# Mean squares of the first residual stream: squares on ScalarE alone, the sums inside TensorE's mean matmuls

## The chip, the cores and the metric

The kernel runs on one core of a Trainium2 chip. The metric is the device time of one execution, in microseconds, as a median over runs. Engines go by the profile's names: PE is TensorE (PEld its weight loads), DVE VectorE, ACT ScalarE, POOL GpSimd, and SP the engine whose queue issues most DMAs.

## The reference

Two decoder layers over 1024 tokens of width 1024, all in f32: the first mixes by differential attention, the second by causal pooling; both also attend to 256 memory tokens. What bears on the change is the normalisation ahead of the first layer.

```python
def rms_norm(x, g):
    xf = x.astype(jnp.float32)
    y = xf * lax.rsqrt(jnp.mean(xf * xf, axis=-1, keepdims=True) + EPS)
    return (y * g.astype(jnp.float32)).astype(x.dtype)
...
    h = x
    mem_n = rms_norm(mem, mem_norm_g)
    for i in range(DEPTH):
        hn = rms_norm(h, ln_g[i])
        ...
            proj = jnp.einsum('bsd,de->bse', hn, attn_w_in[j])
            ...
            y = diff_attention(u, positions, attn_lambda[j], attn_subln_g[j], lambda_init_fn(i))
        ...
        z = jnp.concatenate([y, m], axis=-1) * jax.nn.silu(gate)
        h = h + jnp.einsum('bse,ed->bsd', z, w_out[i])
    return rms_norm(h, final_g)
```

## The kernel before

Activations lie transposed: the model width is on the 128 partitions, in 8 tiles (`d` = 0 to 7), and the tokens are on the free axis in two halves of 512. Half 1 is worked first. Every f32 operand of a projection is split into a high part (`hh`, `wh_...`, made by ScalarE) and a low part (`hl`, `wl_...`, made by VectorE, or by GpSimd and VectorE for weights), and `mm3` issues three matmuls per 128 x 128 x 512 block: L126, L127, L128. A projection of one half is 24 such matmuls.

The row scale of the normalisation, 1/sqrt(mean square), is applied after the projections. So the prologue (`prologue`) does several things at once. It loads x into tiles `xf`, makes `hh` and `hl` of each (`new_hidden`, L498 and L499), and projects q and k of the first head in both halves, in the order k of half 1, q of half 1, k of half 0, q of half 0. It also squares each tile of x and sums the squares over `d` (`accumulate_square`), takes the means by matmuls against a column of 1/1024 (`mean_square`, L251: for each of four groups of 128 tokens one matmul per tile in its list, with one column of output), and forms the inverse root by three Newton steps of small VectorE operations (L225 to L242). The scale is spread over the partitions by matmuls (`row_spread`, L528), copied to `rsb` by ScalarE (L536), and multiplied into the cosine and sine tables (`spread`, L370 and L371). Then the held rotations of q and k run: L761 to L766, then the splits of `kb` (L800, L801) and of `qa` and `qlo` (L781 to L783).

The tables themselves are made in `rope_tables`: angles on VectorE, one sine pass on ScalarE (L560), a DMA to DRAM (L561) and eight DMAs back (L564). ScalarE needs a table load when it goes from sines to exponentials. `lambda_full` (L578 to L584) makes a coefficient for the attention with one exponential (L581).

In `accumulate_square` before, ScalarE squares a tile (L512) or an engine named by `by` does (L510), and the square is added to the first one of its half (L516) by GpSimd, or by VectorE for `d` above 3. In half 1 the last square stays apart (`alone`), so half 1 has a list of two tiles and half 0 a list of one.

The order on TensorE is written by hand (`manual_schedule`): the program order of matmuls is the order of execution. On the other engines and on the DMA queues a scheduler orders the instructions by simulated times, with `high_priority` for the Newton steps, and it orders the whole program anew when a part is changed. After the prologue, score blocks (L849), softmax, transposes and applied weights of twelve heads run interleaved with the projections of the next head, then the memory attention, the output projection, and the second layer.

Of the kernel before, what the change touches and what calls it, by code (L numbers as in the profile page):

```python
# [10 lines left out]
F32 = mybir.dt.float32  # L11
# [3 lines left out]
AF = mybir.ActivationFunctionType  # L15
# [5 lines left out]
P = 128  # L21
# [3 lines left out]
HALF = 512  # L25
# [23 lines left out]
class Trunk:  # L49
# [285 lines left out]
    def prologue(self, pool):  # L335

        nc, a = self.nc, self.a
        xs = {}
        raw = []
        sums = [[], []]  # L340
        w = {}
        held = []

        def load_x(half, c):
            x = pool.tile([P, 2, HALF], F32, tag="eb", bufs=5, name=f"xf{half}{c}")
            nc.sync.dma_start(x, a["x"][half, :, 2 * c : 2 * c + 2, :])
            xs[half, 2 * c], xs[half, 2 * c + 1] = x[:, 0, :], x[:, 1, :]

        def hidden(half, ks):
            for d in ks:  # L350
                self.new_hidden(half, d, xs[half, d], self.ln_g[0])
                self.accumulate_square(
                    pool, xs[half, d], sums[half], d, f"x{half}{d}",
                    (("sq", 2), ("og", 3), ("es", 4)), alone=half == 1, by=None if half else (None, nc.vector)[d % 2],
                    add=nc.vector if d > 3 else None,
                )

        def project(which, half, bank):
            def evac(half, out):
                fn = (self.query_evac, self.key_evac)[which]  # L360
                held.append((half, lambda: fn(0, self.qkv[0][which])(half, out)))

            for _ in self.project(w[which], half, f"{'qk'[which]}0", evac, bank):
                pass

        def spread(half):
            self.keep_spread(half)
            cols = slice(half * HALF, (half + 1) * HALF)
            c, s, r = (t[:, cols] for t in (self.cosr, self.sinr, self.rsb))
            nc.vector.tensor_tensor(c, c, r, op=ALU.mult)  # L370
            nc.vector.scalar_tensor_tensor(  # L371
                s, s, self.cst[:, C_SGN : C_SGN + 1], r, op0=ALU.mult, op1=ALU.mult
            )
            for h, fn in held:
                if h == half:
                    fn()

        load_x(1, 0)
        raw.append(self.load_dma(a["w_in0"][NH], "k0", parts=2))
        for c in range(1, 4):  # L380
            load_x(1, c)
        raw.append(self.load_dma(a["w_in0"][0], "q0"))
        self.rope_tables(pool)
        hidden(1, [0])
        w[1] = self.load_split(raw[0], "k0", dve=320, parts=2)
        hidden(1, range(1, 8))
        w[0] = self.load_split(raw[1], "q0", dve=640)
        for c in range(4):
            load_x(0, c)
        project(1, 1, self.sb)  # L390
        self.row_means(pool, sums[1], 1)
        hidden(0, range(8))
        project(0, 1, self.sb)
        project(1, 0, self.pj)
        spread(1)
        self.row_means(pool, sums[0], 0)
        project(0, 0, self.pj)
        spread(0)
        self.lambda_full(pool)
        self.count = 4 * KT  # L400
# [1355 lines left out]
```

## Time and profile before

| what | value |
|---|---|
| median of 3 runs | 1839.43 us (1836.73 to 1843.68) |
| profiled execution: its own time | 1839.47 us |
| profiled execution: span | 1837.7 us |
| PE busy | 1747.2 us (95%) |
| DVE busy | 1219.4 us (66%) |
| ACT busy | 942.2 us (51%) |
| POOL busy | 640.7 us (35%) |

Times in the trace count from the start of the span. The busy share is an average over stages: what limits the prologue is read from the prologue. PEclk, the granted clock, is 1.00 at 2.4 GHz and 0.50 at 1.2 GHz.

### The profile page before, as it was taken

What the parts mean: (1) busy time and instruction counts of PE and PEld (TensorE: products, weight loads), DVE (VectorE), ACT (ScalarE), POOL (GpSimd) and SP (SyncE); (2) the same over time, 40 slices, a digit from 0 to 9 for tenths busy, and PEclk for the clock granted to TensorE, in tenths of its full rate; (3) what the DMA queues carried; (4) which work ended last, traced back from release to release, by engine and by line L of the source; (5) the groups of instructions that cost most, each with busy time, mean ns of one, the idle gap of its engine ahead of it and who ended that gap; (6) DMA issues with size and microseconds to landing.
All of it is one profiled execution on the core that took longest, in us unless ns stands there. A gap on an engine that the chain in (4) does not pass through costs nothing. (4 is left out here: it accounts for less than half of the span.)

```text
span 1837.7 us, 24949 instructions
## 1 busy us (share of the span) xinstructions
PE 1747.2 (95%) x8634; PEld 1453.9 (79%) x8634; DVE 1219.4 (66%) x2421; ACT 942.2 (51%) x1770; POOL 640.7 (35%) x555
## 2 busy tenths in 40 slices
PE   7799999999999999999989999997999999989997
PEld 5688888888888888888788787875788777767875
DVE  7766676667667667665447677778876767754423
ACT  6667566657657656743246556554533332234422
POOL 4334334343334334333151143500133433413452
PEclk9899999999999999999999999998999999999998
DMA  5011111111111111112462787852312121146542
GB/s 175 33 35 47 39 54 58 35 49 56 35 58 47 35 58 58 36 52 75 149 209 80 241 283 251 285 170 84 111 61 89 61 83 67 54 153 223 164 160 92
DMA packets 83982, 188.68 MB, mean 103 GB/s; under 512 B 9456, under 2 KB 17360, under 8 KB 83856
## 3 DMA queue, kind: packets, MB, share of 16 engines
q1 hardware_dynamic: 81600, 183.08, 30.1%
q10 hardware_dynamic: 2160, 3.75, 0.5%
q8 instruction: 68, 1.11, 0.3%
q14 instruction: 58, 0.48, 0.1%
q0 software_dynamic: 96, 0.26, 0.1%
HBM read 155.29 MB, written 31.77 MB: 102 GB/s over the span
## 5 line engine op out<-in xcount | busy, mean ns | idle before, releaser
L863 ACT ACTIVATE e<-e,st 128x640 f32<-128x640 f32 (+4 forms) x192 | 148.3, 773 | 93.6 <-DVE st L854 92.5
L119 POOL TENSOR_TENSOR wl_o<-wf_o,wh_o 128x288 fp32r<-128x288 f32 (+1 forms) x80 | 110.1, 1377 | 219.9 <-ACT wh_o L116 185.4
L874 POOL TENSOR_SCALAR e<-e,st,coef 128x640 f32<-128x640 f32 (+4 forms) x96 | 89.3, 930 | 169.3 <-DVE st L873 164.6
L1583 DVE TENSOR_TENSOR zr<-zf,zr 128x512 fp32r<-128x512 f32 x132 | 112.4, 866 | 35.4 <-ACT zr L1582 33.7
L119 DVE TENSOR_TENSOR wl_o<-wf_o,wh_o 128x480 fp32r<-128x480 f32 (+1 forms) x80 | 60.3, 754 | 110.6 <-ACT wh_o L116 107.7
L903 ACT CAST wth<-wt 128x512 fp32r<-128x512 f32 (+2 forms) x168 | 71.9, 428 | 107.7 <-PE wt L900 81.4
L1582 ACT CAST zr<-zf 128x512 fp32r<-128x512 f32 x132 | 81.6, 620 | 82.0 <-DMA zf<-z 58.0
L116 ACT CAST wh_o<-wf_o 128x768 fp32r<-128x768 f32 (+1 forms) x80 | 70.1, 876 | 99.4 <-PE ob L127 42.4
L904 DVE TENSOR_TENSOR wtl<-wt,wth 128x512 fp32r<-128x512 f32 (+2 forms) x168 | 83.1, 495 | 55.9 <-ACT wth L903 55.5
L854 DVE CUSTOM_DVE_ANT_0 e<-s,mask 128x512 f32<-128x512 f32 (+2 forms) x192 | 109.2, 583 | 14.5 <-PE s L849 12.4
L849 PE MATMUL s<-kb,qa 128*128 128x512 f32 (+2 forms) x288 | 99.2, 351 | 7.8 <-DVE kb L801 7.2
L126 PE MATMUL ga<-hh,wh_ga 128*128 128x512 f32 x256 | 104.0, 406 | 0.0
L127 PE MATMUL ga<-hl,wh_ga 128*128 128x512 f32 x256 | 100.9, 394 | 0.0
L128 PE MATMUL ga<-hh,wl_ga 128*128 128x512 f32 x256 | 100.9, 394 | 0.0
L849 PE MATMUL s<-kb,qlo 128*128 128x512 f32 (+2 forms) x288 | 98.8, 350 | 0.0
L878 DVE SCALAR_TENSOR_TENSOR e<-e,st,e 128x640 f32<-128x640 f32 (+4 forms) x96 | 80.5, 838 | 14.9 <-POOL e L874 14.2
L126 PE MATMUL k<-hh,wh_k 128*128 128x512 f32 x192 | 80.9, 421 | 8.7 <-ACT wh_k L116 8.7
L126 PE MATMUL oa<-zr,wh_o 128*128 128x512 f32 x192 | 75.8, 395 | 6.2 <-ACT zr L1582 4.2
L128 PE MATMUL oa<-zr,wl_o 128*128 128x512 f32 x192 | 75.3, 392 | 4.7 <-DVE wl_o L119 2.6
L126 PE MATMUL v<-hh,wh_v 128*128 128x512 f32 x192 | 79.6, 414 | 0.0
L127 PE MATMUL k<-hl,wh_k 128*128 128x512 f32 x192 | 76.3, 397 | 3.3 <-DVE hl L499 3.3
L126 PE MATMUL q<-hh,wh_q 128*128 128x512 f32 x192 | 79.2, 413 | 0.0
(1225 smaller groups left out, 5517.9 us busy)
## 6 DMA issues: line engine op xcount, KB each, us to landing
zf<-z SPq DMA_DIRECT2D x132, 256.0 KB
wf_o<-in_w_out SPq DMA_DIRECT2D x64, 384.0 KB
wf_ga<-in_w_in SPq DMA_DIRECT2D x16, 512.0 KB
wf_o<-in_w_out SPq DMA_DIRECT2D x16, 512.0 KB
wf_q<-in_w_in SPq DMA_DIRECT2D x12, 512.0 KB
wf_v<-in_w_in SPq DMA_DIRECT2D x12, 512.0 KB
z<-rs SPq DMA_DIRECT2D x24, 256.0 KB
z<-z SPq DMA_DIRECT2D x24, 256.0 KB
```

Source lines behind the costliest of these rows:

```text
L119: eng.tensor_tensor(wl[:, c], wf[:, c], wh[:, c].bitcast(F32), op=ALU.subtract)
L126: nc.tensor.matmul(out, sh, mh, start=first, stop=False, skip_group_check=more)
L127: nc.tensor.matmul(out, sh, ml, start=False, stop=False, skip_group_check=more)
L128: nc.tensor.matmul(out, sl, mh, start=False, stop=last, skip_group_check=more)
L849: nc.tensor.matmul(sc[m][:, w], q[half][part][:, m, qs], k[kh][:, m, w], start=(part == 0), stop=(part == 1),)
L854: nc.vector.tensor_tensor_reduce(out=es[m][:, lo:hi], in0=sc[m][:, : hi - lo], in1=self.mask[:, S - n + lo : S - n + hi], scale=1.0, scala ...
L863: nc.scalar.activation(es[m][:, :n], es[m][:, :n], AF.Exp, bias=least[m], scale=-1.0, accum_out=st[:, 2, m : m + 1],)
L874: nc.gpsimd.tensor_scalar(es[1][:, :n], es[1][:, :n], st[:, 3, 1:2], self.coef[:, 1:2], op0=ALU.mult, op1=ALU.mult,)
L878: nc.vector.scalar_tensor_tensor(es[0][:, :n], es[0][:, :n], st[:, 3, 0:1], es[1][:, :n], op0=ALU.mult, op1=ALU.add)
L904: nc.vector.tensor_tensor(wl[:, lo:hi], t[:, lo:hi], wh[:, lo:hi].bitcast(F32), op=ALU.subtract)
L1582: nc.scalar.copy(z[:, 0, :], zf)
L1583: nc.vector.tensor_tensor(z[:, 1, :], zf, z[:, 0, :].bitcast(F32), op=ALU.subtract)
```

## The change

All sixteen tiles of x are squared by ScalarE, each into a tile of its own; the additions on GpSimd and VectorE and the squares on VectorE are left out. Both lists handed to `mean_square` have eight tiles, so the sum over `d` is made by TensorE's accumulation within the mean. The sixteen tiles live in eleven buffers borrowed in turn from later users (`homes`), so the last five squares of half 0 reuse buffers that the means of half 1 have read.

```diff
@@ -341,6 +341,8 @@
         w = {}
         held = []
 
+        homes = [("sq", 2)] * 2 + [("og", 3)] * 3 + [("es", 4)] * 4 + [("gate0", 1), ("gate1", 1)]
+
         def load_x(half, c):
             x = pool.tile([P, 2, HALF], F32, tag="eb", bufs=5, name=f"xf{half}{c}")
             nc.sync.dma_start(x, a["x"][half, :, 2 * c : 2 * c + 2, :])
@@ -349,11 +351,10 @@
         def hidden(half, ks):
             for d in ks:
                 self.new_hidden(half, d, xs[half, d], self.ln_g[0])
-                self.accumulate_square(
-                    pool, xs[half, d], sums[half], d, f"x{half}{d}",
-                    (("sq", 2), ("og", 3), ("es", 4)), alone=half == 1, by=None if half else (None, nc.vector)[d % 2],
-                    add=nc.vector if d > 3 else None,
-                )
+                tag, bufs = homes[len(sums[0] + sums[1]) % len(homes)]
+                t = pool.tile([P, HALF], F32, tag=tag, bufs=bufs, name=f"ssqx{half}{d}")
+                nc.scalar.activation(t, xs[half, d], AF.Square)
+                sums[half].append(t)
```

Three places show what moves. The first is TensorE's order at the means of half 0 (`ms_h0`), between the end of k and the start of q of that half; x4 stands for four instructions. Before:

```order
L126 MATMUL k00_426<-hh07_394,wh_k0_229 128x512
L127 MATMUL k00_426<-hl07_395,wh_k0_229 128x512
L128 MATMUL k00_426<-hh07_394,wl_k0_230 128x512
L528 MATMUL bc_h1_451<-cst_72,rsyh_334 128x128 x4
L251 MATMUL ms_h0_489<-inv_d_82,ssqx00_350 128x1 x4
L126 MATMUL q00_508<-hh00_346,wh_q0_285 128x512
```

And in the change, where the eight rows of the means come four times over ahead of q:

```order
L128 MATMUL k00_437<-hh07_406,wl_k0_230 128x512
L529 MATMUL bc_h1_462<-cst_72,rsyh_352 128x128 x4
L251 MATMUL ms_h0_500<-inv_d_82,ssqx00_368 128x1
L251 MATMUL ms_h0_500<-inv_d_82,ssqx01_374 128x1
L251 MATMUL ms_h0_500<-inv_d_82,ssqx02_380 128x1
L251 MATMUL ms_h0_500<-inv_d_82,ssqx03_386 128x1
L251 MATMUL ms_h0_500<-inv_d_82,ssqx04_392 128x1
L251 MATMUL ms_h0_500<-inv_d_82,ssqx05_398 128x1
L251 MATMUL ms_h0_500<-inv_d_82,ssqx06_404 128x1
L251 MATMUL ms_h0_500<-inv_d_82,ssqx07_410 128x1
```

The means of half 0 go from 4 instructions to 32, those of half 1 (ahead of q of half 1) from 8 to 32; nothing else moves on TensorE.

The second place is VectorE at the Newton steps of half 0 (`rsxh`, `rsyh`, `rsuh`), which the spread of half 0 on TensorE waits for. Before, they end ahead of the first use of the tables (`trig_tab`):

```order
L241 SCALAR_TENSOR_TENSOR rsuh_497<-rsuh_497,rsyh_496 128x4
L242 SCALAR_TENSOR_TENSOR rsyh_496<-rsuh_497,rsyh_496 128x4
L370 TENSOR_TENSOR trig_tab_172<-trig_tab_172,rsb_163 128x512
L371 SCALAR_TENSOR_TENSOR trig_tab_172<-trig_tab_172,cst_72,rsb_163 128x512
L762 SCALAR_TENSOR_TENSOR fk01_460<-k01_298,trig_tab_172 128x512
L762 SCALAR_TENSOR_TENSOR fq01_474<-q01_401,trig_tab_172 128x512
```

In the change:

```order
L767 TENSOR_TENSOR fk01_471<-fk01_471,rotk01_470 128x512
L767 TENSOR_TENSOR fq01_485<-fq01_485,rotq01_484 128x512
L802 TENSOR_TENSOR kb01_479<-fk01_471,kb01_479 64x512 x2
L579 TENSOR_TENSOR lam_prod_612<-lam_610 128x128
L581 TENSOR_REDUCE lam_sums_614<-lam_prod_612 128x2
L784 TENSOR_TENSOR qlo0_173<-fq01_485,qa01_493 64x512
L225 TENSOR_SCALAR rsxh_533<-ms_h0_500 128x4
L235 TENSOR_SCALAR rsyh_535<-rsxh_533 128x4
L784 TENSOR_TENSOR qlo0_173<-fq01_485,qa01_493 64x512
L240 TENSOR_TENSOR rsuh_536<-rsxh_533,rsyh_535 128x4
L584 TENSOR_TENSOR coef_71<-lam_sums_614 128x1
L241 SCALAR_TENSOR_TENSOR rsuh_536<-rsuh_536,rsyh_535 128x4
```

The Newton steps of half 0 now come behind half 1's rotation and splits, and among them stand `qlo`, which reads ScalarE's `qa`, and `coef`, which reads ScalarE's exponential. On ScalarE the sines now stand behind the last `hh` of half 0 and ahead of five of the squares, and the exponential with its table load comes behind half 1's `qa`.

The third place is ScalarE in the memory attention of the second layer, far behind the edit: `me` are exponentials of one block of scores, `mwh` transposed weights of the block before, `mq` the cast of a later block's queries, which its load releases. Before:

```order
L684 CAST mwh1010_12446<-mt1010_12441 128x512
L684 CAST mwh1011_12491<-mt1011_12486 128x512
L664 ACTIVATE me111_12473,mst111_12455<-ms1110_12456,mst111_12455 128x256 x2
L664 ACTIVATE me111_12473,mst111_12455<-ms1111_12464,mst111_12455 128x256 x2
L1127 CAST box21_12532<-wf_pmq2_pga14a_12348 128x512
L629 CAST mq100_12544<-mql100_12543 128x512
```

In the change:

```order
L685 CAST mwh1010_12485<-mt1010_12480 128x512
L685 CAST mwh1011_12530<-mt1011_12525 128x512
L1128 CAST box21_12571<-wf_pmq2_pga14a_12387 128x512
L630 CAST mq100_12583<-mql100_12582 128x512
L665 ACTIVATE me111_12512,mst111_12494<-ms1110_12495,mst111_12494 128x256 x2
L665 ACTIVATE me111_12512,mst111_12494<-ms1111_12503,mst111_12494 128x256 x2
```

The cast of `mq` and that of a weight box went ahead of the exponentials.

## Rows read from the trace of the kernel before

**Rows 1.** Windows: busy time (instructions) of each engine, then PEclk, DMA share, GB/s.
```profile
core 0: us, PE busy (x) PEld busy (x) DVE busy (x) ACT busy (x) POOL busy (x), PEclk, DMA share, GB/s
110.00:820.00 710.00, 710.00 (x3825) 605.60 (x3824) 479.77 (x1214) 448.73 (x890) 274.32 (x274) 1.00 0.14 48
```

**Rows 2.** Timeline of PE, prologue: start, duration, instruction, count, [idle before, releaser].
```profile
19.87 0.50 PE L127 MATMUL k<-hl,wh_k 128*128 128x512 f32 x1 [1.85 <-DVE hl L499]
...
21.56 3.03 PE L251 MATMUL ms_h<-inv_d,ssqx 128*128 128x1 f32 x16 [0.96 <-DVE ssqx L516]
24.45 0.77 PE L126 MATMUL q<-hh,wh_q 128*128 128x512 f32 x1
...
32.19 0.39 PE L126 MATMUL k<-hh,wh_k 128*128 128x512 f32 x1
...
38.33 1.16 PE L528 MATMUL bc_h<-cst,rsyh 128*128 128x128 f32 x8 [0.54 <-DVE rsyh L242]
39.32 0.95 PE L251 MATMUL ms_h<-inv_d,ssqx 128*128 128x1 f32 x8
40.13 0.48 PE L126 MATMUL q<-hh,wh_q 128*128 128x512 f32 x1
...
62.17 0.79 PE L849 MATMUL s<-kb,qa 128*128 128x512 f32 x1 [7.24 <-DVE kb L801]
```

**Rows 3.** Timeline of DVE, prologue.
```profile
43.30 0.16 DVE L242 SCALAR_TENSOR_TENSOR rsyh<-rsuh,rsyh 128x4 f32<-128x4 f32 x1
46.38 0.69 DVE L370 TENSOR_TENSOR trig_tab<-trig_tab,rsb 128x512 f32<-128x512 f32 x1 [2.92 <-DMA trig_tab<-trig_all]
...
60.11 0.69 DVE L815 TENSOR_TENSOR vf<-v,rsb 128x512 f32<-128x512 f32 x1
...
61.43 1.40 DVE L801 TENSOR_TENSOR kb<-fk,kb 64x512 fp32r<-64x512 f32 x2
```

**Rows 4.** Timeline of ACT, prologue.
```profile
14.81 1.13 ACT L512 ACTIVATE ssqx<-xf 128x512 f32<-128x512 f32 x2
...
26.67 1.28 ACT L581 ACT_TABLE_LOAD   x1
...
37.64 0.63 ACT L560 ACTIVATE trig<-trig 128x512 f32<-128x512 f32 x1 [1.56 <-DVE trig L559]
...
52.23 2.39 ACT L761 ACTIVATE rotk<-k 32x512 f32<-32x512 f32 x4
55.02 0.62 ACT L781 CAST qa<-fq 64x512 fp32r<-64x512 f32 x1 [0.39 <-DVE fq L766]
```

**Rows 5.** Windows around two stretches at a lower clock, columns as in rows 1.
```profile
22.50:24.00 1.50, 1.50 (x8) 1.50 (x9) 1.50 (x3) 1.47 (x3) 0.81 (x2) 0.50 0.00 0
24.00:28.00 4.00, 4.00 (x11) 3.08 (x12) 4.00 (x7) 3.94 (x6) 0.59 (x1) 0.50 0.34 128
28.90:31.00 2.10, 2.10 (x10) 1.73 (x9) 2.10 (x7) 0.20 (x1) 0.00 (x0) 0.97 0.00 0
60.00:66.50 6.50, 4.33 (x10) 3.42 (x11) 6.03 (x12) 4.01 (x7) 1.27 (x1) 0.50 0.00 0
```

**Rows 6.** Tile view of the squares: count, then ns min/median/max, first and last start.
```profile
L512 ACT ACTIVATE ssqx<-xf x12: 611/614/616, 6.4 to 26.0; 128x512 f32<-128x512 f32 x12
L516 DVE TENSOR_TENSOR ssqx<-ssqx,ssqx x7: 679/684/1766, 15.7 to 35.7; 128x512 f32<-128x512 f32 x7
L516 POOL TENSOR_TENSOR ssqx<-ssqx,ssqx x6: 1264/1608/1740, 8.2 to 23.3; 128x512 f32<-128x512 f32 x6
L510 DVE TENSOR_TENSOR ssqx<-xf x4: 681/683/1750, 16.9 to 29.1; 128x512 f32<-128x512 f32 x4
```

**Rows 7.** Tile view of the low parts in the prologue, columns as in rows 6.
```profile
L499 DVE SCALAR_TENSOR_TENSOR hl<-xf,gains,hh x16: 739/743/1784, 6.5 to 32.9; 128x512 fp32r<-128x512 f32 x16
```

**Rows 8.** Timeline of ACT, DVE and PE in the second layer's memory attention.
```profile
1278.87 0.47 ACT L664 ACTIVATE me<-ms,mst 128x256 f32<-128x256 f32 x1 [0.87 <-DVE mst L661]
...
1281.04 2.19 DVE L670 TENSOR_SCALAR me<-me,mst 128x256 f32<-128x256 f32 x4
...
1281.63 0.62 ACT L629 CAST mq<-mql 128x512 fp32r<-128x512 f32 x1 [0.33 <-DMA mql<-mq]
...
1285.88 0.60 PE L679 MATMUL mt<-cst,me 128*128 128x128 f32 x4
```

## The prediction

> **What bounds the kernel now.** I first read the windows for a stretch in which TensorE never rests. From 110 to 820 us it is busy in all 710.00 us at the full granted clock [rows 1]: time that the prologue (the first 62 us, the only place the diff edits) gives back or loses is neither absorbed nor enlarged there. So I price the prologue by the moment at which TensorE starts the first attention scores, and by the clock it has then.
>
> The timeline of TensorE gives that moment. The first scores start at 62.17, after 7.24 us of waiting for the VectorE instruction that ends the split of `kb` [rows 2]; that one runs from 61.43 to 62.83 [rows 3]. Following it back, VectorE first touched the cosine and sine tables at 46.38, released by their DMA [rows 3]. ScalarE made the sines at 37.64 to 38.27 [rows 4], so DMA out and back cost 46.38 - 38.27 = 8.1 us. The wait behind the 7.24 us is thus a late table, not a late sum of squares. The granted clock was 0.50 from 60 to 66.5 [rows 5] (the 1.2 GHz level, after the 7.24 us of rest): from 62.17 to 66.5 TensorE did half the work of a full clock, a loss of 2.2 us. It is in today's time.
>
> **What is removed.** The view of the squares counts 12 on ScalarE (614 ns), 4 on VectorE (683), and sums of 7 on VectorE (684, up to 1766) and 6 on GpSimd (1608) [rows 6]. VectorE loses 4 x 0.68 + 7 x 0.68 = 7.5 us, GpSimd 9.6 us; neither engine's time is on the path by itself, but three things on the path move.
>
> First, k0 of half 1 ends earlier. Its last three matmuls began at 19.87 because the last `hl` was late by 1.85 us, and ended 0.96 us before 21.56, at 20.6 [rows 2]: 0.73 us from that `hl` to the end. `hl` takes 743 ns in the median and up to 1784 [rows 7], the long ones beside GpSimd's sums. ScalarE's last two squares of half 1 end at 15.94 [rows 4]. Now each `hh` stands ahead of its own square, so the last `hh` ends a square (0.5) sooner, at 15.4; `hl` ends at 16.2 and k0 at 17.0 (18.0 if `hl` still takes the long time).
>
> Second, the sines. ScalarE loaded the exponential's table at 26.67, with 16 `hh`, the rotation copies and 12 squares behind it [rows 4]. The new list ahead of the sines has one square fewer, so they start near 26.1. The tables land at 26.1 + 0.6 + 8.1 = 34.8, and half 1's row scale (below, 36.5 at the earliest) comes later: the table's wait is gone. Two table loads of 1.28 us [rows 4] go as well, hidden.
>
> Third, two waits for sums ahead of the means vanish: the 0.96 at 21.56, and part of the 0.54 at 38.33 [rows 2].
>
> **What is added.** ScalarE's 4 extra squares, 2.5 us, are covered: five squares of half 0 stand behind the sines and are ready by about 29, the means that read them start past 35. Without that cover they would cost the 2.5 us. No DMA is added in the prologue; the loads of x wait for fewer readers.
>
> TensorE gets the bill. In the trace one f32 matmul of the program is two passes: 4 instructions for half 0's means are x8, and 8 for half 1's are x16 [rows 2]. The 32 instructions of each half now are 64 passes, 104 more in all. A pass at the full clock: eight from 39.32 to 40.13, 0.101 us [rows 2]. At the half clock: eight touch the 1.50 us from 22.5, of which seven start there, 0.21 [rows 5]. So a half's means cost between 64 x 0.101 = 6.5 and 64 x 0.21 = 13.6 us, where they took 2.89 and 0.81.
>
> Which price holds? The trace has no such run longer than 16 passes. Those 16 began at the full clock after a stretch of waiting; by 22.5 the clock was 0.50, and it stayed there through the dense q matmuls that began at 24.45 until some 4.5 us later (0.50 over 24 to 28, 0.97 over 28.9 to 31) [rows 5]. The continuous one-column passes from 22.5 to 24.4 had not brought it back. I read this as a row that puts such passes nearer to rest than to work, though the waits before them may have been what lowered the clock. I take 9.0 us for each run: it starts at the full clock, and loses it after about two thirds of its passes (43 x 0.101 + 21 x 0.21 = 8.8). The projection behind each run then costs what q of half 1 cost behind the 16 passes, 24.45 to 32.19 = 7.7, against 5.6 at the full clock (k of half 0, 32.19 to 0.54 before 38.33) [rows 2].
>
> The Trainium skill bears on this choice ("TensorE: Matmul & The Clock Gate", section "What's actually happening"): the throttled level is the default and activity releases it. [...] The trace agrees with the page so far as the 0.50 behind the sixteen passes goes.
>
> **The sum.** TensorE runs in a fixed order. k of half 1 ends 17.0; means of half 1, 9.0: 26.0; q of half 1, 7.7: 33.7; k of half 0, 5.6: 39.3; the spread of half 1's scale, 1.0 (38.33 to 39.32 [rows 2]): 40.3; means of half 0, 9.0: 49.3; q of half 0, 7.7: 57.0; spread, 1.0: 58.0; v of half 1, 5.6: 63.6; half of v of half 0, 2.8: 66.4; then the scores. Beside the last 2.8, VectorE now has `vf` ahead of the rotation's sum and the `kb` split: 0.6 + 0.6 + 1.4 = 2.6 [rows 3], hidden. Scores at 66.4 instead of 62.17 are 4.2 later; but TensorE has not rested, so the 2.2 at the half clock go: +2.0.
>
> The scheduler also exchanged a few instructions far behind, in the memory attention of the second layer. Exponentials that began at 1278.87 now stand on ScalarE behind the cast of `mq`, which waited for its load until 1281.63: they begin near 1282.2, 3.3 late. Their result was ready at 1283.23 and TensorE transposed it, without a wait, at 1285.88 [rows 8]: 2.65 of the 3.3 is slack, and 0.7 falls on TensorE; two VectorE operations put ahead of the scaling make it up to 1.9. I take 1.0; from below I allow -1, since `mq` and a box come earlier. In the last stage some weight loads stand one place later on the DMA queue, behind an activation load. I cost that at nothing, since what moves up is needed as soon; if not, the range's 1 us each way has room for it.
>
> Sum against the profiled execution's own 1839.47: +2.0 + 1.0 = 1842.5. That execution equals the median of the runs shown to 0.04 us, so the median is forecast at **1842.5**.
>
> **The rivals.**
> The clock holds through both runs. For it: passes do follow one another without a gap, and a row cannot tell waits from passes as the cause at 22.5. Then a new wait decides. VectorE's Newton steps for half 0's scale now stand behind `qlo` and `coef`, and `coef` waits for an exponential at the end of ScalarE's list. Sums: 17.0 + 6.5 + 5.6 + 5.6 + 1.0 + 6.5 + 5.6 puts the end of q of half 0 at 47.8. Half 1's spread ends at 35.7, its copy at 36.5 (0.8 by estimate: one ScalarE pass over 512 columns, like the 614 ns squares [rows 6], and its start). From the tables' first use to the copies for half 0's k was 52.23 - 46.38 = 5.85; then 2.4 for these, 4 x 0.635 for `qa`, 1.28 for the table load [rows 4], 0.2 for the exponential, and eight steps of 0.2 on VectorE [rows 3]: 13.9 in all, so the scale is there at 50.4, and TensorE waits 2.6. Behind it 1.0 + 5.6 + 2.8: scores at 59.8. That is -2.4 - 2.2 + 1.0 = -3.6, **1835.9**. In my forecast the same scale is ready at 41.1 + 13.9 = 55.0, before q ends at 57.0, so nobody waits for it.
>
> Slower: the clock is low through both runs and both projections behind them. For it: 0.50 held over 5.5 us across [rows 5]; against: each run follows dense matmuls or bursts of them at the full clock. Runs of 13.6 and projections of up to 2 x 5.6 = 11.2 put the scores at 17.0 + 13.6 + 11.2 + 5.6 + 1.0 + 13.6 + 11.2 + 1.0 + 5.6 + 2.8 = 82.6: +20.4 - 2.2 + 1.0, **1858.7**. It becomes slower by 0.5% (9.2 us) when the four pieces together take over 39.6 us instead of the forecast's 33.4.
>
> The earlier tables decide after all, the added passes lying in what was TensorE's wait of 7.24: this needs the passes to be beside the chain to `kb`, but the row scale that opens this chain comes out of them, so I give it little; it would be at most -7.24 - 2.2, **1830.0**.
>
> **Chances and range.** Forecast (clock falls inside the runs) 0.65, holding times from 1838 to 1847; clock holds through one or both runs 0.22; low throughout or nearly 0.09; the whole wait recovered 0.04. The range 1835.5 to 1849 takes in the second case whole and the third up to the bound of a measurable change; about 0.85 lies inside. A measurement of this kernel tells 0.5% from no change. Faster by more (under 1830.3): 0.04; within: 0.84; slower (over 1848.7): 0.12.
>
> **What would show it.** Right: no table wait on VectorE near the rotation, sines near 26, tables landed before half 1's scale; 64 passes per half, each run 7 to 11 us with the granted clock falling inside; scores at 64 to 69 with no wait ahead of them and the clock full. Wrong: a clock of 1.00 through the passes and a wait of TensorE ahead of the second spread (then the first rival), a k0 of half 1 that still ends past 18, or a change of more than 3 us behind 110 us.

## The result and the profile after

The changed kernel takes **1853.36 us** (median of 4 runs, 1850.34 to 1855.95) against 1840.35 of the kernel before (4 runs): a ratio of 1.0072, interval 1.0053 to 1.0092, or +13.0 us. The forecast was 1842.5 in a range of 1835.5 to 1849: the time is outside. Its profiled execution took 1854.88, with a span of 1853.0. Ratios and intervals here compare the fast executions of two kernels, while a median is over all of a kernel's executions, of which one, of the last kernel with dense sums, was a slow one of 2205.07 us.

Three executions of each kernel were profiled in all. This table gives the start of the same TensorE instruction in each, so the offset grows where time is lost:

| TensorE starts | before, three executions | changed, three executions | means apart |
|---|---|---|---|
| first scores | 62.17, 62.20, 62.49 | 72.12, 70.89, 70.73 | +9.0 |
| last `vt` of the attention | 819.45, 819.15, 818.94 | 829.96, 828.86, 829.12 | +10.1 |
| first `mo` | 970.40, 965.88, 962.33 | 977.64, 976.30, 977.73 | +11.0 |
| last `mo` | 1362.34, 1359.26, 1356.19 | 1371.33, 1366.89, 1369.59 | +10.0 |
| first `oa` of the last stage | 1634.27, 1632.52, 1628.14 | 1644.38, 1639.89, 1641.40 | +10.2 |
| first `ob` of the last stage | 1674.34, 1672.44, 1667.54 | 1687.94, 1683.07, 1683.33 | +13.3 |
| last `ms_rest` | 1820.13, 1818.19, 1813.33 | 1835.19, 1828.66, 1830.37 | +14.2 |

Nine of some fourteen us are there when the scores start, one more by the end of the attention, and about three arise in 40 us at 1640. Between, the same kernel scatters by up to 8 us from one execution to the next, and the means move apart by no more than 1 us, which is within that scatter.

The timeline of TensorE in the changed kernel, which answers to [rows 2]:

```profile
16.81 12.57 PE L251 MATMUL ms_h<-inv_d,ssqx 128*128 128x1 f32 x64
...
29.24 0.77 PE L126 MATMUL q<-hh,wh_q 128*128 128x512 f32 x1
...
37.50 0.39 PE L126 MATMUL k<-hh,wh_k 128*128 128x512 f32 x1
...
42.94 1.05 PE L529 MATMUL bc_h<-cst,rsyh 128*128 128x128 f32 x8
...
43.83 9.22 PE L251 MATMUL ms_h<-inv_d,ssqx 128*128 128x1 f32 x64
...
52.91 0.77 PE L126 MATMUL q<-hh,wh_q 128*128 128x512 f32 x1
...
61.28 1.05 PE L529 MATMUL bc_h<-cst,rsyh 128*128 128x128 f32 x8
62.08 0.48 PE L126 MATMUL v<-hh,wh_v 128*128 128x512 f32 x1
...
72.12 0.50 PE L850 MATMUL s<-kb,qa 128*128 128x512 f32 x1 [1.59 <-DVE kb L802]
...
75.61 0.45 PE L850 MATMUL s<-kb,qa 128*128 128x384 f32 x1 [0.30 <-DVE st L855]
...
83.67 0.50 PE L850 MATMUL s<-kb,qa 128*128 128x512 f32 x1 [1.22 <-DVE st L855]
```

The reader is to see that from 16.8 to 70 TensorE waits for nothing: the 7.24 us of [rows 2] are gone, and the scores are later all the same. The run of half 1 and its q take 12.43 and 8.26 (from start to start), those of half 0 take 9.08 and 8.37. The two runs of 64 in the second and the third execution (the durations shown end 0.14 to 0.15 us behind the start of what follows):

```profile
17.19 10.94 PE L251 MATMUL ms_h<-inv_d,ssqx 128*128 128x1 f32 x64
...
42.60 9.22 PE L251 MATMUL ms_h<-inv_d,ssqx 128*128 128x1 f32 x64
```

```profile
17.01 11.60 PE L251 MATMUL ms_h<-inv_d,ssqx 128*128 128x1 f32 x64
...
42.42 9.88 PE L251 MATMUL ms_h<-inv_d,ssqx 128*128 128x1 f32 x64
```
The windows of the first execution show the clock (columns as in [rows 1], PEclk third from the end):

```profile
16.00:18.00 2.00, 1.76 (x14) 1.68 (x14) 1.92 (x5) 2.00 (x4) 1.19 (x1) 0.99 1.03 420
18.00:20.00 2.00, 2.00 (x11) 2.00 (x10) 2.00 (x4) 2.00 (x4) 0.45 (x1) 0.50 0.70 209
...
34.00:36.00 2.00, 2.00 (x8) 1.55 (x7) 0.00 (x0) 0.00 (x0) 0.00 (x0) 0.74 0.35 71
36.00:43.00 7.00, 7.00 (x33) 5.80 (x32) 0.00 (x0) 2.40 (x5) 0.00 (x0) 1.00 0.00 0
43.00:48.00 5.00, 5.00 (x48) 5.00 (x46) 3.35 (x3) 1.59 (x2) 2.63 (x2) 1.00 0.12 35
48.00:50.00 2.00, 2.00 (x15) 2.00 (x14) 1.81 (x3) 0.00 (x0) 2.00 (x2) 0.68 0.54 178
...
56.00:59.00 3.00, 3.00 (x9) 2.31 (x7) 1.38 (x7) 2.48 (x4) 0.00 (x0) 0.51 0.00 0
59.00:62.00 3.00, 3.00 (x18) 2.60 (x17) 0.98 (x6) 0.75 (x1) 0.00 (x0) 1.00 0.00 0
```

TensorE is busy in every slice. In half 1's run the clock is at its lower level from 18, some 1.2 us after the run began, and stays there through most of the dense q. In half 0's run it falls near 49.

ScalarE and VectorE, by their timelines (they answer to [rows 3, 4]), show why the scores wait for `kb`:

```profile
25.66 0.61 ACT L561 ACTIVATE trig<-trig 128x512 f32<-128x512 f32 x1
...
62.32 2.39 ACT L762 ACTIVATE rotq<-q 32x512 f32<-32x512 f32 x4
64.73 0.59 ACT L537 COPY rsb<-bc_h 128x512 f32<-128x512 f32 x1
```

```profile
44.65 2.33 DVE L371 TENSOR_TENSOR trig_tab<-trig_tab,rsb 128x512 f32<-128x512 f32 x1 [13.09 <-ACT rsb L537]
...
65.35 0.69 DVE L371 TENSOR_TENSOR trig_tab<-trig_tab,rsb 128x512 f32<-128x512 f32 x1 [5.17 <-ACT rsb L537]
...
71.38 1.40 DVE L802 TENSOR_TENSOR kb<-fk,kb 64x512 fp32r<-64x512 f32 x2
```

The sines are early, and VectorE's first use of the tables now waits for the row scale and no longer for the tables' DMA. Half 0's scale was spread on TensorE from 61.28, but its copy stood behind `rotq` until 64.73.

One more thing moved, behind the scores. GpSimd's split of the next head's weights (`wl_k`) came ahead of its first attention step (`e`) in the kernel before and comes behind it now, beside VectorE's step on the same `e`. VectorE and GpSimd, in the kernel before:

```profile
75.04 1.15 DVE L878 SCALAR_TENSOR_TENSOR e<-e,st,e 128x896 f32<-128x896 f32 x1
```

```profile
69.95 2.40 POOL L119 TENSOR_TENSOR wl_k<-wf_k,wh_k 128x1024 fp32r<-128x1024 f32 x1 [8.66 <-ACT wh_k L116]
```

And in the changed kernel:

```profile
79.73 3.28 DVE L879 SCALAR_TENSOR_TENSOR e<-e,st,e 128x896 f32<-128x896 f32 x1 [1.25 <-POOL e L875]
```

```profile
79.66 2.40 POOL L119 TENSOR_TENSOR wl_k<-wf_k,wh_k 128x1024 fp32r<-128x1024 f32 x1
```

The same VectorE step takes 3.28 us in all three executions of the changed kernel and 1.15 in all three of the kernel before.

### The profile page after: what moved, and what is told of

It is laid out like the page before. It is cut to its first block, busy times and chain, and to the rows that moved or that the text cites. A ratio compares the mean times of both kernels' runs of the same rounds, so it can differ in the third digit from the quotient of the medians.

```text
span 1853.0 us, 25140 instructions
## 1 busy us (share of the span) xinstructions
PE 1770.6 (96%) x8738; PEld 1478.0 (80%) x8738; DVE 1208.1 (65%) x2410; ACT 942.2 (51%) x1772; POOL 627.4 (34%) x549
## 4 chain that ended last, share of the span: by engine, by line
PE 78%; DVE 10%; DMA 5%; ACT 4%; issue 2%; POOL 1%; SPq 0%; DVEq 0%; ACTq 0%; POOLq 0%
PE s L850 5%; PE o L924 4%; PE ga L126 3%; PE ga L128 3%; PE ga L127 3%; PE wt L901 2%; PE q L126 2%; PE ob L128 2%; PE ob L126 2%; PE ob L127 2%; PE q L127 2%; PE q L128 2%; DMA zf<-z 2%; PE v L126 2%; PE v L128 2%
## 5 line engine op out<-in xcount | busy, mean ns | idle before, releaser
L119 POOL TENSOR_TENSOR wl_o<-wf_o,wh_o 128x288 fp32r<-128x288 f32 (+1 forms) x80 | 103.6, 1296 | 235.9 <-ACT wh_o L116 192.7
L127 PE MATMUL q<-hl,wh_q 128*128 128x512 f32 x192 | 77.7, 405 | 0.0
```

Source lines behind the costliest of these rows:

```text
L119: eng.tensor_tensor(wl[:, c], wf[:, c], wh[:, c].bitcast(F32), op=ALU.subtract)
L127: nc.tensor.matmul(out, sh, ml, start=False, stop=False, skip_group_check=more)
```

## The experiments

Theory P: the loss is the runs of one-column passes and the lower clock they bring to themselves and to the projection behind. Rival V: the new order on VectorE and ScalarE. Rival L: exchanges far behind the prologue.

**One half at a time.** `hidden` makes tiles of their own for half 1 alone, or for half 0 alone; the other half keeps its sums:

```
if half == 1:          # the other kernel: half == 0
    nc.scalar.activation(t, xs[half, d], AF.Square); sums[half].append(t)
else:
    self.accumulate_square(...)
```

> Half 1 has its eight squares in tiles of their own, summed by TensorE (64 passes); half 0 keeps its sums on VectorE and GpSimd (8 passes). Theory P (the loss is the added one-column passes and the half clock that they bring to themselves and to the projection behind them): the run of half 1 takes 12 to 13 us and its q about 8.3, as in the changed kernel; half 0's means take 0.8 and its q 5.6 to 7, so the first scores come 9 to 12 us earlier than the 72.12 of the changed kernel, at 60 to 63, and the time is about 1841 (1837 to 1845). Rival V (the loss is the new order of VectorE and ScalarE: late Newton steps, late copy of the scale): the order here still has the sines early and one list of Newton steps behind the keys, so scores stay past 68 and the time near 1850. Rival L (most of the 13 us comes from exchanges far behind): scores near 62 and the time still over 1846.

Measured: 1848.34 us, ratio 1.0047 (1.0031 to 1.0062). The run took 12.25 and its q 8.46, as said. But the scores began at 68.48: TensorE waited 4.04 for half 0's Newton steps and 2.07 for `kb`. The run's price held; P's scores and time missed by 5 and 3 us. V's forecast, scores past 68 and a time near 1850, came true in its numbers, by waits that the changed kernel does not have.

> Only half 0 has its eight squares in tiles of their own (64 passes); half 1 is as before the change, and the sines stand behind all squares on ScalarE. Theory P: half 1's 16 passes take 2.9 as before, half 0's run 9 to 13 us and its q 8.3, so scores at 66 to 70 and the time about 1846 (1842 to 1851), between the two kernels. Rival V: this order has the late sines of before, so if order alone made the loss the time is that of before, 1840. Rival L: scores near 62 to 66, time over 1850.

Measured: 1845.58, ratio 1.0049 (1.0030 to 1.0068). Half 0's run took 9.20. The scores began at 62.52, earlier than P's 66 to 70, since half 1 cost less than in the kernel before. The time is in P's range all the same, so what this kernel loses, it loses behind the start of the scores. Half 1's means and its q:

```profile
20.55 1.95 PE L251 MATMUL ms_h<-inv_d,ssqx 128*128 128x1 f32 x16
22.35 0.48 PE L126 MATMUL q<-hh,wh_q 128*128 128x512 f32 x1
```

```profile
18.00:22.00 4.00, 3.93 (x23) 2.98 (x22) 4.00 (x9) 3.98 (x8) 1.14 (x1) 1.00 0.38 139
22.00:28.00 6.00, 6.00 (x30) 5.03 (x30) 6.00 (x22) 5.95 (x11) 0.00 (x0) 1.00 0.28 89
```

Timeline and windows of this kernel: the same 16 passes, with no wait ahead of them, take 1.80 us and keep the clock at 1.00. So 16 passes alone do not bring the 0.50 of [rows 5]; it came where waits like those of [rows 2] stood around them. Only the long run loses the clock by itself.

**Same squares, other sums.** All squares on ScalarE, summed on GpSimd and VectorE (`by=None` in the call before the change).

> All 16 squares on ScalarE in the order of the changed kernel, but summed on GpSimd and VectorE as before, so that TensorE makes 16 and 8 passes. ScalarE's list and VectorE's list of Newton steps are those of the changed kernel. Theory P: no run of 64 passes, so the two runs with their projections take about 2.9 + 7.7 + 0.8 + 5.6 = 17 us instead of 38.1; the scores are then held by the tables and the Newton steps of half 0, behind the last of half 1's copies: they begin at 58 to 65, and the time is 1834 to 1843. Rival V: same order, so the same loss: scores past 68 and time 1849 to 1854. Rival L: scores before 65 and time still over 1846.

Measured: 1846.30, ratio 1.0042 (1.0026 to 1.0057). The scores begin at 62.13, nine us ahead of the changed kernel's mean, where TensorE waits 5.52 for `kb`. This tests V less than was expected: the order came out anew, and ScalarE makes the exponential ahead of the sines, as in the kernel before. ScalarE's timeline:

```profile
27.33 1.28 ACT L581 ACT_TABLE_LOAD   x1
...
31.18 0.63 ACT L560 ACTIVATE trig<-trig 128x512 f32<-128x512 f32 x1
```

Half 0's Newton steps, too, stand among VectorE's first uses of the tables and not behind them. What limits V is the changed kernel's own timeline: from 16.8 to the scores TensorE waits 1.59 us in all. The time missed P's range by 3 us. Rival L's forecast for this kernel, scores before 65 and a time over 1846, came true: 0.42% are lost behind the start of the scores, which no theory here explains (below).

**The same 128 passes, mixed.** Eight of them behind each three matmuls of a projection:

```
for k, _ in enumerate(self.project(...)):
    for i in range(4 * k, 4 * k + 4):      # 4 f32 matmuls = 8 passes
        j, d = divmod(i, KT)
        nc.tensor.matmul(ms[:, j:j+1], sums[d][:, j*P:(j+1)*P], self.inv_d, ...)
```

> The same 128 passes as the changed kernel, but eight of them behind each three 512-column matmuls of a projection: half 1's within q of half 1, half 0's within k of half 0. Theory P (it is the unbroken run that drops the clock, and the low clock that doubles the price): the granted clock stays at or near 1.00, each projection with its passes takes 5.6 + 6.5 = 12.1, q of half 0 takes 5.6 to 6; k of half 1 ends at 17, so the scores begin near 17 + 12.1 + 12.1 + 1 + 5.6 + 1 + 5.6 + 2.8 = 57 (up to 62 where VectorE's and ScalarE's chain to the key split ends later), 10 to 15 us before the changed kernel's 72.12; time 1836 to 1843. Rival I (a one-column pass costs 0.2 us wherever it stands): each projection with its passes takes 19 us, the scores begin past 68 and the time is 1850 or more. Rival C (passes among matmuls lower the clock of the whole stretch): granted clock 0.50 in both projections, 24 us for each, scores past 78 and time over 1858.

Measured: 1854.35, ratio 1.0109 (1.0052 to 1.0167; one of the four executions took 1876.70). Windows over the two projections with their passes, and the first scores in the timeline of TensorE:

```profile
18.00:30.00 12.00, 12.00 (x85) 11.05 (x85) 7.68 (x15) 10.29 (x19) 0.23 (x1) 1.00 0.29 97
30.00:42.00 12.00, 12.00 (x85) 11.00 (x83) 2.23 (x13) 3.29 (x6) 0.00 (x0) 1.00 0.33 72
```

```profile
67.41 0.79 PE L865 MATMUL s<-kb,qa 128*128 128x512 f32 x1 [6.34 <-DVE kb L817]
```

This is the clearest answer on the price: the passes are the same in number, the clock is 1.00 in both windows, and a projection with its 64 passes takes 12.9 (16.59 to 42.38 for two) instead of the 20.7 and 17.5 of the changed kernel. That is near P's 12.1, and I and C fall. P's scores (57, up to 62) and time (1836 to 1843) missed by 5 and 11 us: TensorE now waits 2.74 for Newton steps and 6.34 for `kb`, so the scores start at 67.41, only four us ahead of the changed kernel's mean. Once the passes are cheap, the order on VectorE and ScalarE that V names holds the scores. Nine more us go behind the attention (against the first execution of before, 5.8 later at the last `vt` and 14.7 at the last `ms_rest`).

**The runs doubled.** `mean_square` is called twice for each half.

> The changed kernel with each half's 64 passes made twice, one run behind the other (the first run's result is not read), so 128 passes in a row per half. Theory P (a run this long works at the half clock): the added 128 passes cost 0.19 to 0.2 us each, the first scores come 25 us later than the 72.12 of the changed kernel, at 96 to 98, and the time is about 1878 (1873 to 1883). Rival F (0.50 in the changed kernel came from the waits of k ahead of the run, and a pass costs 0.10): scores at 85, time about 1866.

Measured: 1879.03, ratio 1.0208 (1.0180 to 1.0236); scores at 97.50, +25.4. The windows and the timeline:

```profile
20.00:46.00 26.00, 26.00 (x111) 24.95 (x112) 7.20 (x22) 8.55 (x15) 0.00 (x0) 0.50 0.23 62
...
62.00:84.00 22.00, 22.00 (x92) 20.84 (x92) 6.49 (x21) 7.54 (x12) 0.00 (x0) 0.50 0.01 1
```

```profile
27.52 13.79 PE L251 MATMUL ms_h<-inv_d,ssqx 128*128 128x1 f32 x64
```

No wait stands ahead of or within the second 64, and each costs 0.213 us (13.65 / 64, to the q at 41.17; P said 0.19 to 0.2) at the half clock: the clock stays down as long as the passes last.

**Keys first.** In the changed kernel q of half 1 is evacuated after k of half 0 (`held[2]`, then `held[1]`, `held[3]`).

> The changed kernel, with the evacuation of q of half 1 called only after that of k of half 0, so that the copy of half 0's scale and its key stand ahead of half 1's queries on ScalarE and VectorE where the scheduler's order lets them. All passes stay. Theory P: the two runs and their projections still take 37 to 39 us; only the 1.59 ahead of the scores and some of the 2.1 of waits among them can go: scores at 70 to 72, time 1849 to 1853. Rival V (order of VectorE and ScalarE makes the loss): scores before 66, time 1844 or less.

Measured: 1853.90, ratio 1.0082 (1.0059 to 1.0105). A miss for the small gain I wanted: the wait for `kb` grew to 4.37, scores at 73.43. V's forecast, scores before 66, fails too.

**Dense sums.** Squares in fp32r; TensorE adds eight tiles by the identity, ScalarE copies, eight passes remain; tables' steps with priority and keys first:

```
for i, t in enumerate(sums[half]):
    nc.tensor.matmul(out, ident_r, t, start=(i == 0), stop=(i == KT - 1))
nc.scalar.copy(t, out); sums[half] = [t]
```

> All 16 squares on ScalarE, written as fp32r; TensorE adds the eight of a half with eight 512-column matmuls by the identity, ScalarE copies the sum to SBUF, and 8 one-column passes make the means. The tables' steps have priority, and half 0's key is called ahead of half 1's queries. Theory P: eight dense matmuls cost about 1.9 us at the full clock, means 0.8, projections 5.6 each: k of half 1 ends at 17 to 18, the second spread is done near 43, v ends its half near 51, and the chain from the second spread to the key split ends near 53 to 58; scores at 53 to 58 with the wait of VectorE's kb ahead of them, 4 to 9 us before the 62.17 of the kernel before; time 1829 to 1838 against 1839 to 1840 of before. Rival D (dense adds of this kind, or the waits around the copies, lose the clock as well): scores at 62 or later, time 1840 to 1848. Rival L (exchanges far behind decide): scores before 58 and time still over 1842.

Measured: 1838.36, ratio 0.9988 (0.9975 to 1.0000). Two rows of TensorE's timeline, and a window:

```profile
19.68 1.98 PE L372 MATMUL sum_h<-ssqx,ident_r 128*128 128x512 f32 x8
...
58.76 0.80 PE L866 MATMUL s<-kb,qa 128*128 128x512 f32 x1 [5.09 <-DVE kb L818]
```

```profile
24.00:34.00 10.00, 10.00 (x53) 8.50 (x52) 4.46 (x17) 7.94 (x14) 0.00 (x0) 1.00 0.46 107
```

The adds cost 1.8, q behind takes 5.44, and the clock is full through the means and the projections. What ends last is the chain to `kb`. Scores and time came out just above P's 53 to 58 and 1829 to 1838. Sums, priorities and the order of the keys changed together, so what the dense sums alone are worth is not shown.

> The kernel with dense adds and keys first, in which the two copies of half 0's first key are made by VectorE instead of ScalarE, where they stood behind four qa casts and rotq. Theory P, second part (with the passes gone, the chain to the key split ends last): the wait of 5.09 ahead of the scores shrinks to 2 to 3, scores at 55 to 57 instead of 58.76, time 1834 to 1837 against 1838.4 of that kernel and 1840 of before, a ratio of 0.9965 to 0.9985. Rival D (something else holds the scores, qlo of half 1 or the loads of later heads): scores within 0.7 of 58.8 and the time unchanged.

Measured: 1835.66, ratio 0.9985 (0.9971 to 0.9998). Only the engine of these copies differs (`copy = nc.vector.tensor_copy if h == half == 0 else nc.scalar.copy`); the scores start at 54.55 with 1.27 of wait, a little better than P said. This version beats both kernels, the one before by a margin that its interval barely separates from nothing.

**The stretch at 1640.** Two more executions of each kernel, unchanged:

> The changed kernel once more, for a second profiled execution. Behind the attention the first one lost 1.3 us at 1452, 3.4 between 1640 and 1688 and 1.5 at 1780 against the kernel before, where the granted clock fell after waits that both kernels have. Theory G (where in time such a wait meets the clock's fall is chance): the first scores come again at 72.1 within 0.3, the norms again 10.5 later than before, and the three late pieces differ from those of the first execution by over 1 us in all. Rival R (they belong to the new order of instructions): the same pieces at the same events, within 0.3 us each.

> The kernel before once more, for a second profiled execution. Theory G (where a late wait meets the clock's fall is chance): the first scores again at 62 within 1.5 us, but the stretch from the first oa matmul to the first ob matmul of the last stage, 40.07 us in the first execution, may come out anywhere from 40 to 44. Rival R (the longer stretch belongs to the order of the changed kernel, which took 43.56 and 43.18 us in its two executions): 40.1 within 0.8, with a first wait for zr of 2.0 to 2.5 us.

> The changed kernel a third time, for the stretch from the first oa matmul to the first ob matmul of the last stage, which took 43.56 and 43.18 us in its first two executions against 40.07 and 39.92 of the kernel before. Rival R (the 3.3 us belong to the order of the changed kernel): 43.4 within 0.8 again, with a first wait for zr near 3 us and a granted clock under 0.7 behind it. Theory G (chance): anywhere from 40 to 44. The first scores at 71 to 73, the end of the attention 9 to 11 us later than before.

> The kernel before a third time, for the same stretch. Rival R: 40.0 within 0.8, no fall of the clock in it. Theory G: anywhere from 40 to 44. The first scores at 61 to 63.5.

Measured (one run each): changed 1848.57 and 1850.11, before 1837.82 and 1832.68. First `oa` to first `ob`: changed 43.56, 43.18, 41.93; before 40.07, 39.92, 39.40. These do not overlap, but three against three is thin: the third changed one is outside the band of R, two of before are below that of G, and the other kernels here scatter more (below). The first scores came at 70.89 and 70.73, short of the expected 72.1 and 71 to 73. The fall of the clock at 1452 came again in the second execution of the changed kernel, not in the third, and in the second of before: chance. The 1.5 at 1780 came in two of three, and in none of before, which settles nothing. In the stretch, a fall behind the first wait for `zr` came in two executions of the changed kernel, and the third, without it, is the one of 41.93.

What made that wait longer? Of all queues only q8, of kind instruction, stands differently. In the DMA view, from the issue of the first z load to its first use, the changed kernel has one packet more, and the kernel before has none (its packet lies at 1627, ahead of the loads):

```profile
q8 instruction: 1, 0.02, 1.9%
```

The next two kernels are meant to move that packet (and with it those after it), by idle matmuls in the wait for `mq` (their results are overwritten): `nc.tensor.matmul(t[:, 0, :2], self.ones_r, self.ones_r[:, :2], start=True, stop=True)`, 32 times in the changed kernel, 104 times in the kernel before.

> The changed kernel with 32 more matmuls of two columns in TensorE's wait for mq of the second layer (8.3 us near 1274), whose results are overwritten. The packets on q8 come 256 TensorE instructions apart, 128 matmuls with their weight loads; 32 more put the one that started about 3 us into the last stage's first stretch some 7 us earlier, ahead of the loads of z. Theory Q (that packet delays z): first wait for zr 1.9 to 2.5 us instead of 2.8 to 3.3, the stretch from the first oa to the first ob 39.4 to 41 us instead of 41.9 to 43.6, time 1848 to 1851, about 2.5 under the changed kernel. Rival W (the wait has another cause): wait 2.8 to 3.3, stretch 41.9 to 43.6, time 1850 to 1856 as for the changed kernel.

> The kernel before with 104 more matmuls of two columns in the same wait for mq (8.5 us near 1263), whose results are overwritten; as many as the change adds in passes, but without its squares, means or half clock in the prologue. They take 104 x 0.1 = 10 to 11 us at the half clock, 2 to 3 more than the wait. Theory Q: 69 packets on q8, one of them about 3 us into the last stage's first stretch, first wait for zr 2.8 to 3.3, stretch 41.9 to 43.6, time 1842 to 1845 (2 to 3 from the matmuls, 2.5 from the stretch). Rival W: wait 1.9 to 2.5 and stretch 39.4 to 40.5 as in the kernel before, time 1839 to 1843.

The first wait for `zr` in the timelines of the changed kernel, of the changed kernel with 32 more, and of the kernel before with 104 more:

```profile
1652.01 0.50 PE L126 MATMUL oa<-zr,wh_o 128*128 128x512 f32 x1 [3.32 <-ACT zr L1583]
```

```profile
1651.53 0.49 PE L126 MATMUL oa<-zr,wh_o 128*128 128x512 f32 x1 [2.06 <-ACT zr L1585]
```

```profile
1649.63 0.51 PE L126 MATMUL oa<-zr,wh_o 128*128 128x512 f32 x1 [2.88 <-ACT zr L1584]
```

Both waits came out as Q said: 2.06 without the packet, 2.88 with it, where the kernel before has 1.90 to 2.22. So the packet costs 0.7 to 1.3 us of wait. The stretch took 41.53, above Q's 39.4 to 41, and 42.05, within its 41.9 to 43.6. Both times missed: 1852.36 (ratio 1.0067, 1.0041 to 1.0093) and 1852.99 (1.0076, 1.0048 to 1.0105). The second is far above its range because I priced the idle matmuls at 0.1; the timeline gives 0.213 each, 13.7 us more in all than the 8.48 that the kernel before waits there:

```profile
1249.41 22.18 PE L655 MATMUL ms<-ones_r 128*128 128x2 f32 x104
```

Over all sixteen traces the length of the stretch goes with the clock and not with the packet alone. In the eight with a granted clock of 1.00 throughout it took 39.4 to 41.9 us, in the eight with a fall in it 41.8 to 44.6. Such a fall came in six of the seven with the packet and in two of the nine without it (44.64 in the kernel with half 0 alone, 42.76 in that with the sums elsewhere).

## Why the prediction was wrong

**What held.** k of half 1 ended at 16.8 (forecast 17.0), the sines began at 25.66 (26.1), the table's wait is gone, half 0's scale was ready at 60.2, before q ended at 61.28, and the direction, a run of passes that loses the clock, is shown by the mixed and the doubled kernels. The Trainium skill's rule ("TensorE: Matmul & The Clock Gate", section "What's actually happening"), that the throttled level is the default and activity releases it, agrees with the return of the clock inside the dense q behind each run (0.74 over 34 to 36, 1.00 over 36 to 43). That passes without a wait lose the clock is what the runs add: in the doubled kernel the granted clock is 0.50 from 20 to 46, and passes fill that stretch up to 41.17.

**The step that failed first** is the size of the runs: 9.0 us, "loses it after about two thirds of its passes". Half 1's run took 12.43, 10.80 and 11.46 in three executions, half 0's 9.08, 9.07 and 9.73. At 0.101 and 0.213 per pass a run of 64 lies between 6.5 and 13.6. By an estimate from these two prices, 35 to 41 of half 0's passes ran at the full clock, near my 43, but only 11 to 25 of half 1's: the term was sized for one run and failed for the other. Half 1's run follows a k with waits of 0.16 to 0.29 us, half 0's follows dense matmuls without any; no run tells whether that is the reason. The projections behind took 8.3, 8.3, 7.6 and 8.4, 8.4, 7.7 instead of 7.7. The four pieces were 38.1, 36.5 and 36.6 instead of 33.4: 3.7 more on average. My reason for the price was half wrong too: 16 passes without the waits kept the clock at 1.00.

**Missed wait at the scores.** I wrote that `vf`, the rotation's sum and the split were hidden beside 2.8 us of v. I had not followed ScalarE's list: the copy of half 0's scale stands behind `rotq`, so the scores waited 1.59 for `kb`. With it, the scores are at 71.2 on average against 66.4.

**The credit of 2.2** for a full clock at the scores was not kept. From the first scores to the last `vt` the changed kernel takes 1.2 us longer than the kernel before, on average, and not 2.2 less: TensorE runs into VectorE's maxima (0.30 and 1.22 of waits for `st`, which before does not have at these places). The second of these waits stands behind the VectorE step of 3.28 us. The two kernels reach the first transpose of weights (`wt`) with the same wait for VectorE's `vl`; before and changed:

```profile
85.72 1.26 PE L900 MATMUL wt<-cst,e 128*128 128x128 f32 x8 [2.43 <-DVE vl L825]
```

```profile
96.01 1.71 PE L901 MATMUL wt<-cst,e 128*128 128x128 f32 x8 [2.43 <-DVE vl L826]
```

That is 23.55 and 23.89 us after the first scores: the 2.1 us by which the one step is longer beside GpSimd's split use up the credit. The prediction had no term for where GpSimd's work would fall. The other 1 us up to the last `vt` was not taken apart.

**Costed at nothing: the last stage.** Behind the last `vt` the offset grows by 4.1 us on average, more than the 3 that the prediction named as a sign of its being wrong; 3.1 of it come in one stretch of 40 us. The packet is shown for about 1 us of wait; a fall of the clock behind the longer wait goes with 1.3 to 1.6 more in two of three executions; what makes up the rest stays open. The 1.0 for the memory attention did not show: on average the offset is 10.5 us at the memory scores near 1263 (`ms`) and 10.0 at the last `mo`, within a scatter of several us.

In sum: 4.7 more at the scores, 3.4 through the attention, 3.1 behind it make 11.2, from the forecast's +3.0 to the profiles' +14.2 (medians: +13.0). The rival "low clock throughout" set its threshold at 39.6 us for the four pieces; they stayed below it, and the kernel was slower by 0.7% all the same, by what no case held: the credit that was not kept and the last stage.

**Still open.** The kernel with sums elsewhere starts its scores as early as the kernel before and is 0.42% slower, with no pass added. From the last `vt` to the last `ms_rest` the variants without idle matmuls lost between 1 and 11.5 us against the mean of the three executions of before, which themselves lie 6.3 apart, at waits and falls of the clock that differ by execution. So rival L is not out: how much of the loss behind the scores belongs to the new order of the other engines was not taken apart.

## What to carry to other kernels

A sum over tiles as f32 matmuls of one column cost two passes each here and, in an unbroken run of 64, took the clock away from itself and from the dense work behind it. Mixing the passes into dense matmuls, or adding the tiles first with a few 512-column matmuls by an identity, held the clock; the mixed kernel was 1.1% slower than the kernel before all the same, since another chain then held the scores and more was lost behind the attention. When the wait ahead of a stage vanishes, follow the next chain through each engine's list in order: here the copy behind a longer step was the new bound. Ask too which steps a reordered engine will now run beside. And compare profiled executions of one kernel with each other before explaining a difference of a few us far behind the edit.

## What the runs showed of the hardware

- The same 64 passes cost 0.101 us each between dense matmuls (clock 1.00) and 0.213 in an unbroken run once the clock is at 0.50; TensorE was busy all the time in both. Sixteen passes behind dense matmuls took 1.80 us at 1.00.
- A two-column fp32r matmul with its weight load costs as much at the half clock, 0.213 us, as a pass of an f32 one-column matmul.
- One VectorE step over 128x896 took 3.28 us beside a GpSimd operation of 2.40 and 1.15 without it, in three executions each.
- Packets of 16 KB on queue q8 (68 in the kernel before, 69 after) follow the number of TensorE's instructions, about one for every 128 matmuls with their weight loads. Adding matmuls in the prologue moved one of them, 1600 us later, onto the loads of z, and the first wait behind them is 0.7 to 1.3 us longer. In 9 executions without the packet there, the first wait for `zr` was 1.9 to 2.4 us; in 7 with it, 2.8 to 3.3.
